# Attention: the row maxima of two heads in one pass, in pairs of PSUM banks

## The chip, the core and the metric

The kernel runs on one NeuronCore of a Trainium2 chip. The metric is the device time of one execution in microseconds (us); lower is better. Engines are named as the profile names them: PE is TensorE's matmul, PEld its weight load, DVE VectorE, ACT ScalarE, POOL GpSimd, SP SyncE.

## What is computed

Two layers of a diffusion trunk on 1024 latent tokens (`x`) and 256 context tokens (`ctx`), width 1024. Each layer has a mixer (attention with 8 query heads and 2 key/value heads of 64 channels beside a gated MLP, one output projection) and a SwiGLU FFN. Only the latents' attention and, in layer 0, the context's matter here:

```python
def latent_attention(q, k_all, v_all):        # k_all, v_all: 256 context + 1024 latent tokens
    ...
    def one_block(qblk):
        s = jnp.einsum("bkgqd,bksd->bkgqs", qblk, kt, preferred_element_type=jnp.float32) * scale
        p = jax.nn.softmax(s, axis=-1).astype(vt.dtype)
        return jnp.einsum("bkgqs,bksd->bkgqd", p, vt)
    ...
```

Context queries attend to the context's keys only. The last layer needs no context output.

## The kernel before, in words

Exactness comes from splitting each operand into a rounded part (hi, type fp32r) and the rest (lo): `rnd` (ACT, L118) rounds, `sub_lo` (DVE, L121) takes the rest. All matmuls go through `mm` (L112). SBUF and PSUM are handed out as slots by `Ring`; PSUM is eight slots of one bank each (`BK`), and a slot that is freed goes to the end of the queue. The instructions are written down in the order of the Python code; a list scheduler then sets the order on each engine by that order as priority and by what is ready. Nothing reorders them on the chip.

The attention of a layer works on 16 **units**: two groups of 512 queries by 8 heads. A unit has five **steps** of two key tiles of 128. A step (`step`, L830) makes the transposed logits of two key tiles, four matmuls of 512 columns into two banks: for each key tile Khi by the whole query (`st_k<-qT_p,kh_p` or `kc_p`), then Klo and a row of -1 by the rounded query and the row of maxima (`st_k<-q_p,kl_p`, 65 rows). So the maximum is subtracted inside the product. ACT takes the exponential of each bank by itself (L844, `pt_p<-st_k`), rounds both (`sp_b<-pt_p`, 1024 elements), DVE subtracts (`sp_b<-pt_p,sp_b`). The value products of a step (`values`, six matmuls of 512 columns, two of them 64 wide: `pv_k<-sp_b,vt_p 128*64`) are written two steps later (`run_values(2)`, L894).

The row maxima are made one unit ahead by the generator `prepare` (L698), which is advanced once per step. For a unit it makes the logits with the queries on the partitions: eight matmuls of 512 latent keys (`ml_k`, L718), each into a bank of its own and reduced by a DVE instruction of its own (L719), and four of 256 context keys (`mc_k`, L714), two to a bank with one reduction (L715). The stationary operand has 128 rows, Qhi over Qlo of one head, and the moving one is `[Khi; Khi]`. A last reduction (`m`, L725) joins the chunks, four transposes (`mt_k`, L730) bring the maxima into a row, and ACT rounds that row into the 65th row of `q2` (`q_p<-mt_k`, L731). The second product of the next unit's first step waits for this row. The first unit's `prepare` is advanced twice after each of the last three projections of the queries (L784 to L786) and drained before the first step (L888). In layer 0 a generator `side` runs the context's eight heads between the steps.

Of the kernel before, what the change touches and what calls it, by code (L numbers as in the profile page):

```python
# [10 lines left out]
F32 = mybir.dt.float32  # L11
# [6 lines left out]
P = 128  # L18
# [19 lines left out]
# columns of w_in in the order they are used: u, v (gMLP), k|v, q  # L38
# [3 lines left out]
class Ring:  # L42
    """Slots of one size in SBUF or PSUM, handed out first-freed first."""
# [12 lines left out]
    def part(self, n):  # L56
        """A ring of its own out of n free slots, until it's closed."""
        r = Ring(self.pool, 0, self.pfx, self.words)
        r.queue = [self.queue.pop(0) for _ in range(n)]
        r.up = self  # L60
        r.names = self.names
        return r

    def close(self):
        self.up.queue += self.queue
        self.queue = self.up.queue

# [10 lines left out]
class Share:  # L78
    """A view of a slot that several share; the last one to free it frees the slot."""
# [16 lines left out]
def trunk(ctx: ExitStack, tc, x, xctx, w_mod, b_mod, vecs, gqk, gsg, g_post, w_in, w_sT, w_out,  # L96
# [9 lines left out]
    BK = Ring(ps, 8, "k", 512)  # L106
# [16 lines left out]
    # ---- constants  # L123
# [10 lines left out]
    one_v = cst.tile([P, 2, 2], F32, name="one_v")     # a column of ones, as the first of two or as the second  # L134
# [7 lines left out]
    fm = cst.tile([P, 2, 2, 4, KT], F32, name="fm")   # [layer][x/ctx][a_mix, b_mix, a_ffn, b_ffn]  # L142
# [16 lines left out]
    # ---- modulation vectors  # L159
# [9 lines left out]
    def mods_first():  # L169
        """Shift and scale of the first norm, both streams at once: products, then columns."""  # L170
# [130 lines left out]
    def norm_early(xt):  # L301
        """Normed and transposed, before the modulation is known."""
# [53 lines left out]
    class Lag:  # L356
        """Work whose emission waits until n more pieces of work came behind it."""
# [13 lines left out]
    # ---- weights as a rounded part and the exact rest  # L371
# [21 lines left out]
    # ---- one layer  # L393
# [8 lines left out]
    class HT:  # L402
        """Normed activations, features on partitions, as stationary tiles: hi/lo [128, kt, 128] per token tile."""
# [6 lines left out]
        def next_l(self):  # L410
            """One more pair of tiles."""
# [49 lines left out]
    def gmlp_mix(l, vs, up, ws):  # L461
        """m = (W_s v + b_s) * u, in place of u."""
# [20 lines left out]
    def head_norm(src, nt, nh, tabA, tabB):  # L483
        """RMS norm over each head's 64 channels with gain and rotation folded into tabA/tabB; f32 result page."""
# [21 lines left out]
    def layer(l):  # L506
# [3 lines left out]
        # -- norms, gMLP  # L510
# [85 lines left out]
        for g, (kind, prs) in enumerate(groups):  # L596
            n = 2 * len(prs)
            vs[g] = [(PG.get([n, PC], F32R, "vh"), PG.get([n, PC], F32R, "vl")) for _ in range(2)]
            for k, pr in enumerate(prs):
# [37 lines left out]
        for kind, pr in [("c", 0)] + [("l", i) for i in range(4)]:  # L637
# [36 lines left out]
            v = PG.get([2, KVH, 3, HD], F32R, "vt")      # [Vhi | 1 | Vlo]  # L674
# [10 lines left out]
        # -- attention: units of (kind, group of query tiles, head)  # L685
# [12 lines left out]
        def prepare(u):  # L698
            """Row maxima of the logits, and [Qhi; max] as a moving operand; in steps."""
# [4 lines left out]
            mx = sm.tile([P, 4, 3], F32, name="mx", tag="mx")  # L704
# [809 lines left out]
```

## Time and profile before

| what | value |
| --- | --- |
| median of 3 runs | 2771.4 us (2771.33 to 2777.08) |
| the profiled execution | span 2767.1 us from its first to its last instruction; no time of its own is given |
| attention of layer 0, first to last value product | 303.7 to 556.7 us |
| attention of layer 1 | 1758.5 to 1989.8 us |
| busy share of the span, PE, DVE, ACT, POOL | 98%, 71%, 45%, 16% |

The profile gives times of one execution, in us from its first instruction. The median lies 4.3 us above the span: what lies outside the first and last instruction. A matmul's recorded duration runs from its start to the modelled end of its results, so it overlaps the next one; how fast matmuls follow each other is read from merged rows of several (the row's length less one duration, over the count less one). The same holds for ACT and DVE instructions, which overlap a little where they stand back to back.

### The profile page before, as it was taken

How to read it: one execution, taken by the hardware profiler on the slowest of the kernel's cores; microseconds unless marked ns; L12 is line 12 of the kernel's file. 1: busy time of each engine (PE TensorE's matmuls, PEld its weight loads, DVE VectorE, ACT ScalarE, POOL GpSimd, SP SyncE). 2: the span in 40 equal slices, each digit the busy share in tenths (PEclk: the TensorE clock that was granted, in tenths of full speed). 3: DMA queues.
4: the chain of work that ended last, by engine and by line, in shares of the span. 5: the costliest groups of instructions: out<-in, count | busy, mean ns of one | idle time of the engine just before them, and what ended most of it. 6: DMA issues, size and time to landing. Idle time of an engine off the chain costs nothing.

```text
span 2767.1 us, 36916 instructions
## 1 busy us (share of the span) xinstructions
PE 2719.3 (98%) x14257; PEld 2267.2 (82%) x14257; DVE 1970.5 (71%) x2806; ACT 1235.2 (45%) x2055; POOL 444.8 (16%) x463
## 2 busy tenths in 40 slices
PE   7999999999999999999999999999998999999998
PEld 4999777688888788888899999777787888888887
DVE  6775788857888897865688556888758666666544
ACT  5323788845333223411276323688744333335111
POOL 1112000003232332000010002000013232330003
PEclk9999999999999999999999999999999999999999
DMA  7330000233532434742376410001232212225223
GB/s 276 121 124 32 3 14 20 79 110 108 205 136 107 153 137 138 257 170 97 106 240 225 139 56 32 5 8 36 91 130 90 78 71 82 92 77 190 84 77 114
DMA packets 91614, 298.14 MB, mean 108 GB/s; under 512 B 20431, under 2 KB 21263, under 8 KB 86318
## 3 DMA queue, kind: packets, MB, share of 16 engines
q1 hardware_dynamic: 91438, 295.78, 30.5%
q8 instruction: 112, 1.84, 0.3%
q14 instruction: 64, 0.52, 0.1%
HBM read 249.96 MB, written 45.71 MB: 107 GB/s over the span
## 4 chain that ended last, share of the span: by engine, by line
PE 88%; ACT 4%; DMA 3%; DVE 3%; issue 1%; POOL 1%; SPq 0%; DVEq 0%; POOLq 0%; ACTq 0%
PE fi_k L112 34%; PE fo_k L112 19%; PE pz_k L112 6%; PE op_k L112 6%; PE pv_k L112 6%; PE st_k L112 4%; PE pq_k L112 4%; PE ml_k L112 2%; PE pkv_k L112 2%; ACT pt_p L115 1%; ACT sp_b L118 1%; PE mg_k L112 1%; PE hT_k L334 1%; PE m_k L112 1%; DMA wraw_p<-in_w_in_dram 1%
## 5 line engine op out<-in xcount | busy, mean ns | idle before, releaser
L112 PE MATMUL fi_k<-blk_p,fw_p 128*128 128x512 f32 x2640 | 608.0, 390 | 0.3 <-ACT blk_p L118 0.3
L112 PEld LDWEIGHTS fi_k<-blk_p,fw_p 128*128 128x128 f32 x2640 | 496.3, 188 | 104.7 <-issue 0.9
L112 PE MATMUL pv_k<-sp_b,vt_p 128*128 128x512 f32 (+2 forms) x1008 | 277.5, 394 | 5.0 <-DVE sp_b L121 4.0
L118 ACT ACTIVATE fw_p<-fir_b 128x512 fp32r<-128x512 f32 x200 | 126.1, 631 | 319.5 <-PE fi_k L112 304.1
L112 PE MATMUL fi_k<-blk_b,fw_p 128*128 128x512 f32 x1056 | 251.8, 395 | 0.4 <-DVE y_p L972 0.4
L286 POOL TENSOR_SCALAR rs<-ss 128x1 f32<-128x1 f32 x74 | 24.7, 333 | 1333.5 <-DVE ss L968 607.0
L112 PEld LDWEIGHTS fi_k<-blk_b,fw_p 128*128 128x128 f32 x1056 | 201.4, 191 | 42.9 <-DVE y_p L972 0.8
L121 DVE TENSOR_TENSOR sp_b<-pt_p,sp_b 128x1024 fp32r<-128x1024 f32 (+1 forms) x168 | 200.3, 1195 | 26.8 <-ACT sp_b L118 24.8
L112 PE MATMUL fo_k<-foh_p,foh_p 128*128 128x512 f32 x704 | 218.4, 390 | 0.0
L112 PE MATMUL fo_k<-fol_p,foh_p 128*128 128x512 f32 x704 | 218.0, 389 | 0.0
L112 PE MATMUL fo_k<-foh_p,fol_p 128*128 128x512 f32 x704 | 217.9, 389 | 0.0
L112 PEld LDWEIGHTS pv_k<-sp_b,vt_p 128*128 128x128 f32 (+1 forms) x1008 | 162.4, 170 | 62.9 <-DVE sp_b L121 11.4
L1246 DVE TENSOR_TENSOR acc_b<-fo_k,acc_b 128x512 f32<-128x512 f32 x176 | 113.1, 685 | 140.1 <-PE fo_k L112 140.1
L719 DVE TENSOR_REDUCE mx<-ml_k 128x1 f32<-128x512 f32 x256 | 168.1, 685 | 39.9 <-PE ml_k L112 39.2
L118 ACT ACTIVATE foh_p<-fo_b 128x1024 fp32r<-128x1024 f32 x88 | 90.6, 1058 | 227.4 <-PE fo_k L112 122.8
L112 PE MATMUL pz_k<-winh_p,hTl_b 128*128 128x256 f32 x1024 | 187.6, 285 | 0.2
L115 ACT ACTIVATE pt_p<-st_k 128x512 f32<-128x512 f32 (+1 forms) x336 | 180.6, 590 | 14.9 <-PE st_k L112 13.8
L121 DVE TENSOR_TENSOR fw_p<-fir_b,fw_p 128x512 fp32r<-128x512 f32 x200 | 176.7, 884 | 11.2 <-ACT fw_p L118 9.0
L234 DVE SCALAR_TENSOR_TENSOR macc_p<-wm_p,cT,macc_p 128x1024 f32<-128x1024 f32 x128 | 171.8, 1356 | 14.3 <-DMA wm_p<-in_w_mod_dram 11.8
L118 ACT ACTIVATE sp_b<-pt_p 128x1024 fp32r<-128x1024 f32 (+1 forms) x168 | 175.8, 1046 | 1.7
L112 PEld LDWEIGHTS pz_k<-winh_p,hTl_b 128*128 128x128 f32 x1024 | 161.0, 193 | 2.9 <-issue 0.9
L112 PEld LDWEIGHTS fo_k<-foh_p,foh_p 128*128 128x128 f32 x704 | 131.8, 188 | 28.7 <-DVE gp_p L247 0.9
(261 smaller groups left out, 5362.0 us busy)
## 6 DMA issues: line engine op xcount, KB each, us to landing
wm_p<-in_w_mod_dram SPq DMA_DIRECT2D x112, 512.0 KB
fir_b<-in_w_fi_dram SPq DMA_DIRECT2D x40, 1024.0 KB
fir_p<-in_w_fi_dram SPq DMA_DIRECT2D x52, 512.0 KB
hid<-hid_p SPq DMA_DIRECT2D x44, 512.0 KB
fo_b<-hid SPq DMA_DIRECT2D x44, 512.0 KB
fo_b<-in_w_fo_dram SPq DMA_DIRECT2D x44, 512.0 KB
wraw_p<-in_w_in_dram SPq DMA_DIRECT2D x28, 512.0 KB
for_p<-in_w_fo_dram SPq DMA_DIRECT2D x22, 512.0 KB
```

The lines of the kernel that those rows point to most:

```text
L112: nc.tensor.matmul(o, lhsT, rhs, start=start, stop=stop)
L115: A.activation(out=o, in_=i, func=f, **kw)
L118: A.activation(out=o, in_=i, func=AF.Copy)
L121: V.tensor_tensor(out=o, in0=i, in1=hi.bitcast(F32), op=ALU.subtract)
L234: V.scalar_tensor_tensor(out=accs[v].t, in0=w.t, scalar=cT[:, v, kt:kt + 1], in1=accs[v].t, op0=ALU.mult, op1=ALU.add)
L286: nc.gpsimd.tensor_scalar(out=y, in0=src, scalar1=float(eps), scalar2=1.0, op0=ALU.add, op1=ALU.mult)
L334: nc.tensor.transpose(bk.t[:, k, :], xs.t[:, (4 * q + k) * P:(4 * q + k + 1) * P], idn)
L719: V.tensor_reduce(out=mx[:, b, i:i + 1], in_=bk.t, axis=AX.X, op=ALU.max)
L1246: V.tensor_tensor(out=a, in0=bks[h].t, in1=a, op=ALU.add)
```

## The change

The line numbers of the changed kernel are those before plus 46 in the helpers, and a few more further down (`mm` is L158, `rnd` L164, `sub_lo` L167).

- PSUM becomes one tile of eight banks (`Banks`); `two` hands out an even bank and the next one as a pair. During the steps banks 6 and 7 are set apart for the value products (`PV`), so that three pairs are left for logits, maxima and transposes.
- The queries of the odd head of a pair are stored as lo over hi instead of hi over lo. `prepare` then works for two heads at once: head 0 on rows 0 to 63 of the array, head 1 on rows 64 to 127, Qhi by Khi alone, each into its own bank of a pair. One DVE instruction reduces both banks (1024 elements). The number of matmuls is the same.
- `prepare` is made once per pair of heads, for the pair that follows, with ten chunks and a last step; it is advanced once per step over the ten steps of two units. Eight transposes stand together, and one ACT instruction rounds the maxima of both heads (1024 elements of one partition); the copy of Qhi into `q2` is two ACT instructions instead of one.
- A step's logits lie in a pair of banks, and one ACT instruction takes the exponential of both.

```diff
-            if h % 2 == 0:
-                q2[kind, g, h // 2] = t = PG.get([2, nqb * P], F32R, "q2")
-                rnd(t.t[:HD], qp.t[:HD].bitcast(F32))
-            for n, (b, i) in enumerate(chunks):
+            q2[kind, g, h // 2] = t = PG.get([2, nqb * P], F32R, "q2")
+            for j in range(2):
+                rnd(t.t[:HD, j], qp.t[j * HD:(j + 1) * HD, j].bitcast(F32))
+            half = [slice(0, HD), slice(HD, P)]
+            for b, i in chunks:
                 if b == "c":
-                    bk = BK.get([2, CTX], F32, "mc")
+                    bk = BK.two([2, 2, CTX])
+                    for n in range(2):
+                        for j in range(2):
+                            mm(bk.t[:, j, n], qp.t[half[j], j, (2 * i + n) * P:(2 * i + n + 1) * P], kc.t[half[j], 0, kv, :], True, True)
+                    V.tensor_reduce(out=mx[:, :, 2 * i:2 * i + 2, 2], in_=bk.t, axis=AX.X, op=ALU.max)
+                else:
+                    bk = BK.two([2, 512])
                     for j in range(2):
-                        mm(bk.t[:, j], qp.t[:, h % 2, (2 * i + j) * P:(2 * i + j + 1) * P], kc.t[:, 0, kv, :], True, True)
-                    V.tensor_reduce(out=mx[:, 2 * i:2 * i + 2, 2], in_=bk.t, axis=AX.X, op=ALU.max)
-                else:
-                    bk = BK.get([512], F32, "ml")
-                    mm(bk.t, qp.t[:, h % 2, b * P:(b + 1) * P], kh[kv].t[:, i * 512:(i + 1) * 512], True, True)
-                    V.tensor_reduce(out=mx[:, b, i:i + 1], in_=bk.t, axis=AX.X, op=ALU.max)
+                        mm(bk.t[:, j], qp.t[half[j], j, b * P:(b + 1) * P], kh[kv].t[half[j], i * 512:(i + 1) * 512], True, True)
+                    V.tensor_reduce(out=mx[:, :, b, i], in_=bk.t, axis=AX.X, op=ALU.max)
                 bk.free()
-                if n % 2 == 1 and n < len(chunks) - 1:
-                    yield
+                yield
...
-                bks = [BK.get([nq], F32, "st") for _ in range(2)]
+                bk = BK.two([2, nq])
                 for k in range(2):
                     kt = 2 * k2 + k
-                    mm(bks[k].t, kslice(0, kv, kt), qa, True, False)
-                    mm(bks[k].t, kslice(1, kv, kt), qb, False, True)
-                    act(pt.t[:, k, :], bks[k].t, AF.Exp)
-                for bk in bks:
-                    bk.free()
+                    mm(bk.t[:, k], kslice(0, kv, kt), qa, True, False)
+                    mm(bk.t[:, k], kslice(1, kv, kt), qb, False, True)
+                act(pt.t, bk.t, AF.Exp)
+                bk.free()
...
+            PV = BK.part([6, 7])
             for n, u in enumerate(units):
-                pre = prepare(units[n + 1]) if n + 1 < len(units) else iter(())
+                if n % 2 == 0:
+                    pre = prepare(units[n + 2]) if n + 2 < len(units) else iter(())
```

Outside the attention and the end of the projection of the queries, the instructions of every engine stand in the same order as before. Two places inside show what moves.

DVE at the start of layer 1's attention, from the last norm of the queries (`qss`) to the first joined maximum (`m`). Before:

```order
L489 TENSOR_REDUCE qss<-sq_p_16426 128x8
L496 TENSOR_TENSOR qr_p_16433<-pq_k_16377,tab_p_15213 128x512
L498 TENSOR_TENSOR sq_p_16426<-pq_k_16377,tab_p_15213 128x8x32 x2
L715 TENSOR_REDUCE mx<-mc_k_16454 128x2
L500 TENSOR_TENSOR qr_p_16433<-qr_p_16433,sq_p_16426 128x512
L715 TENSOR_REDUCE mx<-mc_k_16458 128x2
L502 TENSOR_TENSOR qr_p_16433<-qr_p_16433,rs 128x512
L725 TENSOR_REDUCE m_16462<-mx 128x4
```

With the change, the same stretch (L769 reduces a pair of `ml` banks, L764 a pair of `mc` banks, L774 joins):

```order
L535 TENSOR_REDUCE qss<-sq_p_15202 128x8
L542 TENSOR_TENSOR qr_p_15209<-banks,tab_p_14039 128x512
L544 TENSOR_TENSOR sq_p_15202<-banks,tab_p_14039 128x8x32 x2
L769 TENSOR_REDUCE mx<-banks 128x2
L546 TENSOR_TENSOR qr_p_15209<-qr_p_15209,sq_p_15202 128x512
L769 TENSOR_REDUCE mx<-banks 128x2
L548 TENSOR_TENSOR qr_p_15209<-qr_p_15209,rs 128x512
L769 TENSOR_REDUCE mx<-banks 128x2
L167 TENSOR_TENSOR qst_p_15215<-qr_p_15209,qst_p_15215 128x4x128
L769 TENSOR_REDUCE mx<-banks 128x2
L764 TENSOR_REDUCE mx<-banks 128x2x2 x2
L774 TENSOR_REDUCE m_15272<-mx 128x8
```

Four reductions of `ml` pairs and one `sub_lo` come ahead of the joined maximum, and all six reductions take two banks.

PE at a border of two units of layer 1, around the transposes of the maxima (`idr,m`). Before (`st_k` are logits, `pv_k` values, `q_p` is `q2`):

```order
L112 MATMUL st_k_16780<-qT_p_16031,kh_p_15340 128x512
L730 MATMUL mt_k_16741<-idr,m_16739 1x128 x4
L112 MATMUL st_k_16781<-qT_p_16031,kh_p_15340 128x512
L112 MATMUL pv_k_16688<-sp_b_16728,vt_p_15785 128x512
L112 MATMUL pv_k_16688<-sp_b_16728,vt_p_15785 64x512
L112 MATMUL pv_k_16688<-sp_b_16728,vt_p_15785 128x512
L112 MATMUL st_k_16755<-q_p_16630,kc_p_15344 128x512
```

With the change, a border of two pairs of heads (`kc_p,qT_p` is the last quad of `mc`, `kh_p,qT_p` the next pair's first `ml`):

```order
L158 MATMUL banks<-kc_p_14168,qT_p_15142 128x256 x4
L158 MATMUL banks<-sp_b_15840,vt_p_14394 128x512
L158 MATMUL banks<-sp_b_15840,vt_p_14394 64x512
L158 MATMUL banks<-sp_b_15840,vt_p_14394 128x512 x2
L158 MATMUL banks<-sp_b_15840,vt_p_14394 64x512
L158 MATMUL banks<-sp_b_15840,vt_p_14394 128x512
L158 MATMUL banks<-qT_p_15142,kc_p_14168 128x512 x2
L780 MATMUL banks<-idr,m_15892 1x128 x8
L158 MATMUL banks<-kh_p_14164,qT_p_14976 128x512 x2
L158 MATMUL banks<-sp_b_15858,vt_p_14512 128x512
L158 MATMUL banks<-sp_b_15858,vt_p_14512 64x512
L158 MATMUL banks<-sp_b_15858,vt_p_14512 128x512
L158 MATMUL banks<-q_p_15700,kc_p_14168 128x512 x2
```

Eight transposes stand where four stood, one `ml` pair and three value products are left between them and the product that reads the row of maxima, and logits of the next step no longer stand among them.

## Rows read from the trace of the kernel before

**Rows 1.** The page: the span, and busy time of each engine.

```profile
span 2767.1 us, 36916 instructions
...
PE 2719.3 (98%) x14257; PEld 2267.2 (82%) x14257; DVE 1970.5 (71%) x2806; ACT 1235.2 (45%) x2055; POOL 444.8 (16%) x463
```

**Rows 2.** Busy time by stretch: attention of both layers, then their starts.

```profile
core 0: us, PE busy (x) PEld busy (x) DVE busy (x) ACT busy (x) POOL busy (x), PEclk, DMA share, GB/s
303.00:557.00 254.00, 248.33 (x1148) 180.29 (x1146) 212.24 (x295) 219.23 (x349) 0.00 (x0) 1.00 0.13 33
1758.00:1990.00 232.00, 230.04 (x1029) 166.30 (x1028) 197.31 (x266) 196.58 (x296) 0.00 (x0) 1.00 0.12 34
293.00:303.00 10.00, 8.28 (x30) 5.71 (x30) 7.05 (x14) 6.26 (x11) 1.84 (x2) 0.66 0.00 0
1745.00:1758.00 13.00, 11.99 (x46) 8.20 (x45) 9.48 (x17) 9.62 (x16) 1.83 (x2) 0.74 0.00 1
```

**Rows 3.** The tiles ml_k and mc_k: duration ns min/median/max, first and last start.

```profile
L112 PE MATMUL ml_k<-kh_p,qT_p x256: 387/396/755, 277.6 to 1967.3; 128*128 128x512 f32 x128
L112 PE MATMUL mc_k<-kc_p,qT_p x128: 274/282/366, 292.3 to 1969.6; 128*128 128x256 f32 x128
L112 PE MATMUL mc_k<-kc_p,qTc_p x16: 278/281/580, 296.0 to 375.8; 128*128 128x256 f32 x16
```

**Rows 4.** Timeline, steady steps of layer 1: start us, length us, instruction, [idle before].

```profile
1850.83 0.63 PE L112 MATMUL mc_k<-kc_p,qT_p 128*128 128x256 f32 x4
...
1852.76 1.07 ACT L118 ACTIVATE q_p<-qT_p 64x1024 fp32r<-64x1024 f32 x1
...
1853.71 1.06 ACT L118 ACTIVATE sp_b<-pt_p 128x1024 fp32r<-128x1024 f32 x1
...
1854.22 1.54 PE L112 MATMUL pv_k<-sp_b,vt_p 128*128 128x512 f32 x6
1854.69 0.68 DVE L719 TENSOR_REDUCE mx<-ml_k 128x1 f32<-128x512 f32 x1
1855.28 1.22 DVE L121 TENSOR_TENSOR sp_b<-pt_p,sp_b 128x1024 fp32r<-128x1024 f32 x1
...
1855.60 0.62 PE L112 MATMUL st_k<-qT_p,kh_p 128*128 128x512 f32 x2
```

**Rows 5.** Timeline, a border of two units in layer 1.

```profile
1838.02 2.39 DVE L121 TENSOR_TENSOR sp_b<-pt_p,sp_b 128x1024 fp32r<-128x1024 f32 x2
...
1840.40 1.28 DVE L719 TENSOR_REDUCE mx<-ml_k 128x1 f32<-128x512 f32 x2
...
1840.82 0.60 PE L730 MATMUL mt_k<-idr,m 128*1 128x128 f32 x4
...
1841.46 0.59 ACT L118 ACTIVATE q_p<-mt_k 1x512 fp32r<-1x512 f32 x1 [2.31 <-PE mt_k L730]
...
1842.19 0.64 PE L112 MATMUL st_k<-q_p,kc_p 65*128 65x512 f32 x2
...
1842.63 1.58 ACT L115 ACTIVATE pt_p<-st_k 128x512 f32<-128x512 f32 x3 [0.59 <-PE st_k L112]
```

**Rows 6.** Timeline, the start of layer 1's attention.

```profile
1743.76 0.28 PE L112 MATMUL pq_k<-winh_p,hTl_b 128*128 128x256 f32 x1
...
1743.88 0.79 PE L776 MATMUL qTp_k<-idr,qst_p 128*128 128x128 f32 x8
...
1744.71 0.69 DVE L489 TENSOR_REDUCE qss<-sq_p 128x8 f32<-128x512 f32 x1 [1.23 <-ACT sq_p L115]
...
1748.96 0.16 DVE L725 TENSOR_REDUCE m<-mx 128x4 f32<-128x12 f32 x1
...
1749.18 0.60 PE L730 MATMUL mt_k<-idr,m 128*1 128x128 f32 x4 [0.17 <-DVE m L725]
...
1750.45 0.80 PE L112 MATMUL st_k<-q_p,kc_p 65*128 65x512 f32 x1
```

**Rows 7.** Waits of PE in the steps, layer 1: us in total, times, longest.

```profile
PEld pv_k L112 <- DVE sp_b L121: 5.0, 12, 1.0
PEld st_k L112 <- ACT q_p L118: 3.1, 14, 0.4
```

**Rows 8.** The same waits in layer 0.

```profile
PEld pv_k L112 <- DVE sp_b L121: 6.5, 11, 1.9
PEld st_k L112 <- ACT q_p L118: 5.5, 18, 0.9
```

More of the change, by code (lines that the diff above doesn't have):

```diff
@@ L66, in close, with __init__, get, part @@
         self.queue = self.up.queue
+class Banks:
+    def __init__(self, pool, n):
+        self.t = pool.tile([P, n, 512], F32, name="banks")
+        self.queue = list(range(n))
+    def get(self, shape, dt=F32, name="t"):
+        return Bank(self, [self.queue.pop(0)], shape)
+    def part(self, at):
+        r = Banks.__new__(Banks)
+        r.t, r.up, r.queue = self.t, self, list(at)
+        self.queue = [i for i in self.queue if i not in at]
+        return r
+    def close(self):
+        self.up.queue += self.queue
+    def two(self, shape):
+        q = self.queue
+        i = min((i for i in q if i % 2 == 0 and i + 1 in q), key=lambda i: max(q.index(i), q.index(i + 1)))
+        q.remove(i)
+        q.remove(i + 1)
+        return Bank(self, [i, i + 1], shape)
+class Bank:
+    def __init__(self, banks, at, shape):
+        self.banks, self.at = banks, at
+        n = int(np.prod(shape)) // len(at)
+        t = banks.t[:, at[0], :n] if len(at) == 1 else banks.t[:, at[0]:at[0] + 2, :n]
+        if len(at) == 1 and len(shape) == 2:
+            t = t.rearrange("p (a b) -> p a b", b=shape[1])
+        if len(shape) == 3:
+            t = t.rearrange("p (a b c) -> p a b c", b=shape[1], c=shape[2]) if len(at) == 1 else t.rearrange(
+                "p a (b c) -> p a b c", c=shape[2])
+        self.t = t
+    def free(self):
+        self.banks.queue += self.at
+        self.t = None
 class Slot:
@@ L105, in trunk @@
     BG = Ring(sb, NBIG, "b", 4096)
-    BK = Ring(ps, 8, "k", 512)
+    BK = Banks(ps, 8)
     dma = nc.sync.dma_start
@@ L720, in prepare @@
                 bk.free()
-                if n % 2 == 1 and n < len(chunks) - 1:
-                    yield
+                yield
             if lat:
-                m4 = sm.tile([P, 4], F32, name="m4", tag="m4")
+                m4 = sm.tile([P, 2, 4], F32, name="m4", tag="m4", bufs=2)
                 V.tensor_reduce(out=m4, in_=mx, axis=AX.X, op=ALU.max)
             else:
-                m4 = mx[:, :, 2]
-            bk = BK.get([nqb, P], F32, "mt")
-            for b in range(nqb):
-                nc.tensor.transpose(bk.t[0:1, b, :], m4[:, b:b + 1], idn)
@@ L731, in prepare @@
-            rnd(q2[kind, g, h // 2].t[HD:HD + 1, h % 2, :], bk.t[0:1].rearrange("p a t -> p (a t)"))
+                m4 = mx[:, :, :, 2]
+            bk = BK.two([2, nqb, P])
+            for j in range(2):
+                for b in range(nqb):
+                    nc.tensor.transpose(bk.t[0:1, j, b, :], m4[:, j, b:b + 1], idn)
+            rnd(t.t[HD:HD + 1], bk.t[0:1].rearrange("p j a t -> p j (a t)"))
             bk.free()
@@ L757, in layer @@
                 rf = r.t.rearrange("p a h d -> p (a h) d")
-                rnd(st.t[:, :, 0:HD], rf)
-                sub_lo(st.t[:, :, HD:2 * HD], rf, st.t[:, :, 0:HD])
+                sv = st.t.rearrange("p (g h) (x d) -> p g (h x) d", h=2, x=2)
+                rg = rf.rearrange("p (g h) d -> p g h d", h=2)
+                rnd(sv[:, :, 0::3], rg)
+                sub_lo(sv[:, :, 1:3], rg, sv[:, :, 0::3])
                 r.free()
@@ L853, in values @@
                     if k2 == 0:
-                        pv[u] = BK.get([nq], F32, "pv")
+                        pv[u] = PV.get([nq], F32, "pv")
                     bk = pv[u]
@@ L872, in side @@
                     q = []
-                    drain(prepare(u))
+                    if h % 2 == 0:
+                        drain(prepare(u))
                     yield
@@ L895, in attention @@
                     next(more, None)
-                drain(pre)
+                if n % 2 == 1:
+                    drain(pre)
                 done(u)
@@ L900, in attention @@
             run_values(0)
+            PV.close()
             return outs
```

2 lines of the change are left out of this document (1 added, 1 removed).

## The prediction

> **What bounds the kernel now.** First the page: PE is busy 2719.3 of the span's 2767.1 us, DVE 71%, ACT 45% [rows 1]. That is the whole program, and the change touches its two attentions, so the next view is busy time by stretch [rows 2]. In layer 1's attention PE is busy 230.04 of 232 us, ACT 196.58 and DVE 197.31; in layer 0's 248.33, 219.23 and 212.24 of 254. The granted clock is 1.00 in both, the upper level (2.4 GHz). So PE bounds each stage, with two engines close behind at 85%: time saved on PE counts, but not without limit. The waits say where PE stood: for the rest of the probabilities (`sp_b`) 5.0 us in layer 1 and 6.5 in layer 0, for the row of maxima (`q_p`) 3.1 and 5.5 [rows 7, 8].
>
> Durations overlap, so costs are pitches from merged rows. Six value products take 1.54 us and one 0.39, so one follows another after (1.54 - 0.39) / 5 = 0.23 us; four `mc` take 0.63 and one 0.28: 0.12 us [rows 3, 4]. 512 columns at 2.4 GHz are 0.213 us; the other 0.017 I take as the change of weights.
>
> **Half the array.** The number of matmuls stays. 256 `ml` and 144 `mc`, of which 400 are listed [rows 3], now use 64 rows each, and by the order on PE 119 pairs of 512 columns and 67 of 256 stand with opposite halves next to each other; 24 stand alone. If the halves run side by side, the second of a pair costs only about 0.017: 119 x 0.213 + 67 x 0.103 = **-32.2 us**. If they don't, nothing is saved. No row of this trace shows two matmuls in different rows, so this is the largest unknown. What speaks for overlap is only that nothing in the operands forbids it: other rows, other banks. I take overlap.
>
> The Trainium skill ("TensorE: Matmul & The Clock Gate", Part 3) says that matmuls in different row groups run at once, 3.07 times faster for four of them; my estimate from that page is a tenth of a matmul for each further one, which would make the saving 31.2 us. No run here shows it yet.
>
> **DVE and ACT.** A reduction of 512 takes 0.60 us in a row of two (1.28 - 0.68) and a subtraction of 1024 1.17 (2.39 - 1.22) [rows 4, 5]; I take 1.17 for a reduction of two banks, between 1.13 and 1.20. So 256 x 0.60 become 128 x 1.17, 2% less. An exponential of 512 takes 0.53 in a row at most (1.58 / 3) [rows 5], a pass of 1024 elements 0.95 (1853.71 - 1852.76) [rows 4], so merging two gains ACT 0.1 us. Neither bounds: 0 us. The split copy of Qhi costs ACT a start more per head, hidden as long as ACT has its 15% free.
>
> **Start of each attention.** Here DVE decides. From the last norm of the queries to the joined maximum it works from 1744.71 to 1749.12 without a break [rows 6]. By the order it now has six reductions of two banks and one `sub_lo` there in place of two reductions: 6 x 1.17 + 0.60 - 2 x 0.60 = +6.4 us. Eight transposes for four: four take 0.60, so at most 0.60 more, taken 0.5; one rounding of 1024 for 512: 1.06 - 0.59 = +0.47 [rows 4, 5]. Against that eight transposes of queries that came after the first logits now lie in the gap: -0.8 [rows 6]. The `ml` and `mc` drawn into the gap are counted once, with the pairs. +6.6 per layer, **+13.2 us**. It can't be hidden behind other work: in the 13 us after the last projection PE has little to do even now and runs at a mean clock of 0.74 (0.66 in layer 0) [rows 2].
>
> **Borders.** Seven borders of head pairs per layer replace fifteen of heads. At one, the last `mc` quad is followed by a reduction (1.17), the join (0.16) and the transposes; ahead of that reduction on DVE may stand up to a whole subtraction (1.17). From the last matmul's start to the maxima that is 0.28 + 1.17 + 0.16 + 0.06 to 1.17 more, 1.67 to 2.84. The order gives PE six value products and two logits in that time: 0.12 + 8 x 0.23 = 1.96. PE waits 0 to 0.88. Then ACT rounds 1024 elements (1.06, behind up to 0.95 of another pass) while PE has only an `ml` pair and three value products (4 x 0.23 = 0.92): 0.2 to 1.15. The middle of both is 1.1 us, 14 times: +15.4. Gone are the waits of before for `q_p`, 3.1 + 5.5 x 14/18 = 7.4 (four of layer 0's 18 I count to the context, which stays) [rows 7, 8]. Net **+8.0 us**, bounds -4.6 and +21.
>
> **Pairs of banks.** One exponential waits for four products where each waited for two: 0.46 us later at most. The value products stand two steps later, which hides it but for the waits on `sp_b` that exist: 12 + 11 times [rows 7, 8], 23 x 0.46 = 10.6 as the upper bound, 0 as the lower. Layer 1's waits are short against the two steps' slack, so I take a quarter: **+2.5 us**.
>
> **Clock.** At the starts PE loses about (1 - 0.74) x 13 + (1 - 0.66) x 10 = 6.8 us to the lower level, 1.2 GHz [rows 2]. A longer gap can prolong that; bounds 0 and 6.8, taken **+2 us**, since the gaps grow by half and hold little PE work.
>
> Sum: -32.2 + 13.2 + 8.0 + 2.5 + 2 = -6.5 us on a span of 2767.1, so 2760.6. The median of the runs lies 4.3 us above that span: **2765 us**.
>
> **The rivals.**
>
> *Each switch drains the array* (slower). By the order the 400 half-row matmuls stand in 160 runs among full ones, 320 switches. Rows show that a change in columns costs nothing: two of the six value products at 0.23 are 64 wide [rows 4]. Of rows they show nothing: the 65-row logits follow each other in 0.64 - 0.39 = 0.25 [rows 5], but are still more than half. If the array must be empty before a switch, it costs up to 0.39 - 0.23 = 0.16 us, 51 us in all. It decides from 6.5 / 320 = 0.02 us on. At the middle, 0.08 a switch, a tenth of them in gaps: +23 - 6.5, 2788 us. For it: no row excludes it. Against it: nothing else in the trace that alternates shapes stalls. 0.20.
>
> The Trainium skill ("TensorEngine Tiling (Array Packing)", Key Properties) states that changing the tiling mode drains TensorE, which is this rival's rule; the 64-wide value products are such a change in columns, and the trace shows no drain at them, so that row speaks against the rule.
>
> *The halves don't overlap.* The saving is 0; start-ups and borders gain the matmuls moved into them (2 x 1.8 and 14 x 0.23), and neither clock nor exponentials cost anything, since PE stays further behind: 13.2 - 3.6 + 15.4 - 3.2 - 7.4 = +14.4, 2786 us. This is also the case in which the change does not do what it says. 0.13.
>
> *The new waits are hidden.* Borders at their lower bound (-4.6), pairs of banks and clock 0: -32.2 + 13.2 - 4.6 = -23.6, which would be 2748; with the two close engines in the way rather 2754. Against it: ACT has a pass of 1024 in its way at most times. 0.15.
>
> **How the numbers follow.** A difference under 0.2% (5.5 us) can't be told from none. The forecast has 0.52 and a range of its own, 2757 to 2772: the borders at 0.5 or 1.6 us, the clock at 0 or 6.8. Its middle lies at the edge of 0.2%, so about 0.29 of it is faster, 0.22 the same, the rest slower. With hidden waits (nearly all faster) and the two slow rivals, whose low ends reach down to no change (switches under 0.04 us; borders well covered): faster 0.43, same 0.30, slower 0.27. The range goes from 2752 to 2788, through most of the slow rivals; a full drain lies outside it.
>
> **What the new profile would show.** Right: the second of an `ml` pair starts within 0.03 us of the first, and a logits product after a pair not later than 0.25 after its last. PE's waits for `q_p` at borders about 0.6 us, and for `m` 0.4, 14 times; the first transpose of layer 1 some 12 us after the last `pq` instead of 5.4; ACT and DVE busier as a share, PE less. Wrong: pairs with 0.23 between starts (no overlap); 0.05 to 0.16 more ahead of or behind each half-row run (drain); waits on `sp_b` of more than 10 us per layer (the pairs of banks, or DVE, became the bound).

## The result and the profile after

The change made the kernel slower: 2799.1 us median (2797.6 to 2803.4) against 2772.8; the ratio is 1.0101, 95% interval 1.0086 to 1.0117. That lies outside the range, beyond the rival in which switches drain the array (2788 us). The profiled execution has a span of 2795.8 us, 28.7 more than before [rows 1]. Its time was 2797.6, 1.8 us above the span; the 4.3 us that the prediction put between span and median is more than lies outside the first and last instruction, so before's profiled run was probably some 2.5 us faster than its median.

The page of the changed kernel:

```profile
span 2795.8 us, 36626 instructions
...
PE 2737.9 (98%) x14257; PEld 2242.9 (80%) x14257; DVE 1958.9 (70%) x2626; ACT 1235.4 (44%) x1887; POOL 438.6 (16%) x463
```

PE is still the bound, with 18.6 us more busy time than before for the same number of matmuls. Where the 28.7 us came in is read from three marks in each layer: the last matmul of the query projections (`winh_p`), and the first and last value product (`sp_b,vt_p`). In the table, "start" is the time from the first of these marks to the second, "steps" from the second to the third, for the kernels that the text needs (before, the change, and the experiments that follow):

| us | before | change | e1 | e3 | e8 | e11 |
| --- | --- | --- | --- | --- | --- | --- |
| start, layer 0 | 12.15 | 25.51 | 23.94 | 27.01 | 22.60 | 14.32 |
| steps, layer 0 | 252.56 | 254.44 | 245.54 | 267.35 | 249.19 | 246.26 |
| start, layer 1 | 14.71 | 23.94 | 21.29 | 24.36 | 22.21 | 13.37 |
| steps, layer 1 | 230.98 | 236.04 | 224.77 | 253.67 | 229.90 | 224.76 |

The two starts take 22.6 us more, the steps 6.9; the rest of the program differs by 0.8 the other way. (Where layer 0's projections end varies by up to 4.4 us from before in these kernels, and the stretch between the layers by up to 5; these are not explained here. The profiled execution was the slowest of nine for e8, 3.5 us over its median, and the fastest of eight for e11, 3.7 us under it.)

A steady piece of layer 1 after the change, from the timeline:

```profile
1846.44 0.39 PE L158 MATMUL banks<-q_p,kl_p 65*128 65x512 f32 x1
1846.76 0.19 PEld L158 LDWEIGHTS banks<-kh_p,qT_p 64*128 64x128 f32 x2 [0.36 <-issue]
1846.76 0.51 PE L158 MATMUL banks<-kh_p,qT_p 64*128 64x512 f32 x2
...
1847.20 1.24 PEld L158 LDWEIGHTS banks<-sp_b,vt_p 128*128 128x128 f32 x6 [0.25 <-issue]
1847.20 1.67 PE L158 MATMUL banks<-sp_b,vt_p 128*128 128x512 f32 x6
```

Two matmuls of 64 rows take 0.51 us together, so they run side by side. But the first comes 0.32 after the product ahead of it, not 0.23; the value products come 0.44 after the pair, not 0.23; and six of them take 1.67, not 1.54 [rows 4]. The load of the first half-row matmul's weights (PEld) starts with the matmul, not one matmul ahead: 0.001 us before it, in the kernel of e1 below 0.229 us (medians of 88 places). PEld's waits in the steps of layer 1 and of layer 0, where "issue" means that nothing in the profile was waited for:

```profile
PEld banks L158 <- issue: 31.9, 106, 0.4
PEld banks L158 <- ACT sp_b L164: 4.2, 12, 0.6
PEld banks L158 <- DVE sp_b L167: 2.8, 3, 1.0
PEld banks L158 <- ACT q_p L164: 2.5, 8, 0.6
PEld banks L158 <- ACT pt_p L161: 2.1, 6, 0.5
...
PEld banks L158 <- issue: 28.9, 100, 0.4
PEld banks L158 <- ACT pt_p L161: 5.0, 11, 1.1
PEld banks L158 <- ACT sp_b L164: 4.1, 11, 0.4
PEld banks L158 <- ACT q_p L164: 2.5, 7, 0.7
```

Rows of the same view of the kernel before, layer 1:

```profile
PEld ml_k L112 <- ACT pt_p L115: 5.7, 22, 0.4
...
PEld pv_k L112 <- ACT pt_p L115: 2.0, 9, 0.3
PEld st_k L112 <- ACT pt_p L115: 2.0, 10, 0.2
...
PEld pv_k L112 <- ACT sp_b L118: 1.3, 3, 0.7
```

PE's wait for `sp_b` on DVE fell from 5.0 to 2.8 in layer 1, the wait for `q_p` from 3.1 to 2.5 in layer 1 and from 5.5 to 2.5 in layer 0 [rows 7, 8], those for `pt_p` in layer 1 from 9.7 to 2.1. The wait on data that rose most is that for `sp_b` on ACT, from 1.3 to 4.2 in layer 1. The data waits together fell; what is new in the steps is 206 times "issue".

The start of layer 1, timeline of the changed kernel:

```profile
1758.36 0.28 PE L158 MATMUL banks<-winh_p,hTl_b 128*128 128x256 f32 x1
...
1759.31 0.69 DVE L535 TENSOR_REDUCE qss<-sq_p 128x8 f32<-128x512 f32 x1 [0.45 <-ACT sq_p L161]
...
1768.84 2.36 DVE L764 TENSOR_REDUCE mx<-banks 128x4 f32<-128x1024 f32 x2 [1.25 <-PE banks L158]
...
1771.23 0.18 DVE L774 TENSOR_REDUCE m<-mx 128x8 f32<-128x24 f32 x1
...
1771.99 1.87 PE L780 MATMUL banks<-idr,m 128*1 128x128 f32 x8
...
1773.90 1.01 ACT L164 ACTIVATE q_p<-banks 1x1024 fp32r<-1x1024 f32 x1 [4.34 <-PE banks L780]
...
1774.96 1.22 PE L158 MATMUL banks<-q_p,kc_p 65*128 65x512 f32 x2 [0.38 <-ACT q_p L164]
...
1776.40 0.63 PE L158 MATMUL banks<-q_p,kl_p 65*128 65x512 f32 x1
...
1776.83 0.63 PE L158 MATMUL banks<-qT_p,kh_p 128*128 128x512 f32 x1
...
1782.30 1.05 PE L158 MATMUL banks<-sp_b,vt_p 128*128 128x512 f32 x2
```

The maxima are joined 13.0 us after the last projection instead of 5.4, and the first transpose comes at 13.6 [rows 6]. Busy time and granted clock by stretch (columns as in [rows 2]):

```profile
1758.00:1763.00 5.00, 3.57 (x30) 2.72 (x29) 4.38 (x8) 2.90 (x6) 1.83 (x2) 1.00 0.00 0
1763.00:1768.00 5.00, 2.35 (x15) 1.54 (x14) 4.59 (x5) 1.33 (x3) 0.00 (x0) 0.69 0.00 0
1768.00:1773.00 5.00, 4.12 (x12) 2.31 (x13) 2.53 (x3) 1.54 (x3) 0.00 (x0) 0.50 0.00 0
1773.00:1778.00 5.00, 4.62 (x13) 3.00 (x11) 1.23 (x1) 3.40 (x4) 0.00 (x0) 0.50 0.00 0
1778.00:1783.00 5.00, 4.03 (x11) 2.16 (x11) 2.57 (x3) 3.86 (x4) 0.00 (x0) 0.50 0.00 0
1783.00:1788.00 5.00, 5.00 (x17) 3.35 (x17) 3.79 (x4) 2.92 (x3) 0.00 (x0) 0.77 0.00 0
```

PE is busy 2.35 of 5 us while DVE works, then runs at 0.50, the lower level (1.2 GHz), until the first value products are through. There a logits product follows the one ahead of it after 0.43 us (1776.40 to 1776.83) instead of 0.23. By the trace's clock records the lower level lasted 20.4 us here and 23.9 in layer 0; before, 6.8 us in each.

### The profile page after: what moved, and what is told of

Its sections match the earlier page's. It is cut to its first block, busy times and chain, and to the rows that moved or that the text cites. A ratio compares the mean times of both kernels' runs of the same rounds, so it can differ in the third digit from the quotient of the medians.

```text
span 2795.8 us, 36626 instructions
## 1 busy us (share of the span) xinstructions
PE 2737.9 (98%) x14257; PEld 2242.9 (80%) x14257; DVE 1958.9 (70%) x2626; ACT 1235.4 (44%) x1887; POOL 438.6 (16%) x463
## 4 chain that ended last, share of the span: by engine, by line
PE 91%; DVE 3%; ACT 2%; DMA 2%; issue 1%; POOL 1%; SPq 0%; DVEq 0%; POOLq 0%; ACTq 0%
PE banks L158 89%; PE banks L380 1%; PE banks L780 1%; ACT pt_p L161 1%; DMA wraw_p<-in_w_in_dram 0%; ACT sp_b L164 0%; PE banks L829 0%; POOL rs L333 0%; DVE sp_b L167 0%; DVE mx L769 0%; DMA wor_p<-in_w_out_dram 0%; DMA wm_p<-in_w_mod_dram 0%; ACT ov_p L161 0%; DMA ov_p<-rd0l 0%; PE banks L709 0%
## 5 line engine op out<-in xcount | busy, mean ns | idle before, releaser
L158 PE MATMUL banks<-blk_p,fw_p 128*128 128x512 f32 x2640 | 608.4, 390 | 0.3 <-ACT blk_p L164 0.3
L158 PEld LDWEIGHTS banks<-blk_p,fw_p 128*128 128x128 f32 x2640 | 496.5, 188 | 105.0 <-ACT blk_p L164 0.9
L158 PE MATMUL banks<-winh_p,hTl_b 128*128 128x256 f32 x1792 | 332.8, 286 | 1.0 <-DVE hTl_b L167 0.5
L158 PEld LDWEIGHTS banks<-winh_p,hTl_b 128*128 128x128 f32 x1792 | 283.8, 193 | 5.0 <-issue 2.1
L158 PE MATMUL banks<-sp_b,vt_p 128*128 128x512 f32 (+2 forms) x1008 | 276.0, 404 | 2.4 <-DVE sp_b L167 1.8
L164 ACT ACTIVATE fw_p<-fir_b 128x512 fp32r<-128x512 f32 x200 | 126.0, 631 | 318.8 <-PE banks L158 303.5
L158 PE MATMUL banks<-winl_p,hTl_b 128*128 128x256 f32 x896 | 254.7, 284 | 0.0
L158 PE MATMUL banks<-blk_b,fw_p 128*128 128x512 f32 x1056 | 250.2, 393 | 2.7 <-DVE y_p L1029 2.7
L332 POOL TENSOR_SCALAR rs<-ss 128x1 f32<-128x1 f32 x74 | 21.3, 288 | 1368.3 <-DVE ss L1025 638.2
L158 PEld LDWEIGHTS banks<-blk_b,fw_p 128*128 128x128 f32 x1056 | 199.9, 190 | 44.9 <-DVE y_p L1029 3.1
L167 DVE TENSOR_TENSOR sp_b<-pt_p,sp_b 128x1024 fp32r<-128x1024 f32 (+1 forms) x168 | 198.7, 1195 | 48.7 <-ACT sp_b L164 48.3
L158 PEld LDWEIGHTS banks<-sp_b,vt_p 128*128 128x128 f32 (+1 forms) x1008 | 160.2, 171 | 81.5 <-issue 24.5
L158 PE MATMUL banks<-foh_p,foh_p 128*128 128x512 f32 x704 | 218.3, 390 | 0.0
L158 PE MATMUL banks<-fol_p,foh_p 128*128 128x512 f32 x704 | 217.9, 389 | 0.0
L158 PE MATMUL banks<-foh_p,fol_p 128*128 128x512 f32 x704 | 217.9, 389 | 0.0
L769 DVE TENSOR_REDUCE mx<-banks 128x2 f32<-128x1024 f32 x128 | 155.9, 1220 | 51.6 <-PE banks L158 36.8
L164 ACT ACTIVATE foh_p<-fo_b 128x1024 fp32r<-128x1024 f32 x88 | 90.7, 1060 | 227.3 <-PE banks L158 151.2
L167 DVE TENSOR_TENSOR fw_p<-fir_b,fw_p 128x512 fp32r<-128x512 f32 x200 | 176.6, 883 | 11.3 <-ACT fw_p L164 9.0
L164 ACT ACTIVATE sp_b<-pt_p 128x1024 fp32r<-128x1024 f32 (+1 forms) x168 | 172.4, 1039 | 3.6
```

The source lines that it names most:

```text
L158: nc.tensor.matmul(o, lhsT, rhs, start=start, stop=stop)
L164: A.activation(out=o, in_=i, func=AF.Copy)
L167: V.tensor_tensor(out=o, in0=i, in1=hi.bitcast(F32), op=ALU.subtract)
L332: nc.gpsimd.tensor_scalar(out=y, in0=src, scalar1=float(eps), scalar2=1.0, op0=ALU.add, op1=ALU.mult)
L769: V.tensor_reduce(out=mx[:, :, b, i], in_=bk.t, axis=AX.X, op=ALU.max)
```

## The experiments

Two theories stood against each other after the result. **S**: each passage between full-row and half-row use of the array costs PE time, more than the overlap returns; and the start of each attention is late. **B**: the later maxima at borders and the merged exponentials cost the time, and the halves are a gain.

**e1, full rows.** Two heads at once, pairs of banks and the order on PE stay; the array is used whole.

```diff
-            half = [slice(0, HD), slice(HD, P)]
+            half = [slice(0, P), slice(0, P)]
```

> The changed kernel, but each maxima matmul uses all 128 rows again (Qhi over Qlo, or Qlo over Qhi, by [Khi; Khi]); pairs of banks, paired reductions, merged exponentials, two heads at once and the order on PE stay. Theory S (each passage between full-row and half-row use of the array costs time, about 0.10 us in and 0.20 us out, and the overlap of the halves gives back 0.21 per pair): in the steps the trace of the changed kernel has 39.9 us at 139 runs' borders against 26.9 us of overlap, so 13 us go, and some 4 to 8 more at the two start-ups: 2778 to 2783 us. Rival B (the later maxima at borders and the merged exponentials cost the time, the halves are a gain): the overlap is lost, 2810 to 2826 us, or nothing changes, 2799.

Measured: 2773.9 us, ratio 1.0021 (1.0011 to 1.0031): as S has it, and below its range. B falls. In the profile the steps take 20.2 us less than with the change, the starts 4.2. A steady piece:

```profile
1829.80 0.40 PE L158 MATMUL banks<-q_p,kl_p 65*128 65x512 f32 x1
...
1830.03 0.63 PE L158 MATMUL banks<-kh_p,qT_p 128*128 128x512 f32 x2
...
1830.50 1.54 PE L158 MATMUL banks<-sp_b,vt_p 128*128 128x512 f32 x6
```

Theory S had counted 13 us in the steps, for the way into each run and out of it; it had no term for the matmul behind each run (the table of e3).

**e2, half rows in the kernel before.** One edit to before's `ml` and `mc` (the line for `ml` is shown, that for `mc` is narrowed alike); it leaves Qlo by Khi out of the maxima.

```diff
-                    mm(bk.t, qp.t[:, h % 2, b * P:(b + 1) * P], kh[kv].t[:, i * 512:(i + 1) * 512], True, True)
+                    mm(bk.t, qp.t[:HD, h % 2, b * P:(b + 1) * P], kh[kv].t[:HD, i * 512:(i + 1) * 512], True, True)
```

> The kernel before with one edit: its maxima matmuls use rows 0 to 63 alone (Qhi by Khi), so the product Qlo by Khi is left out of the maxima. Nothing can overlap, and nothing else changes; by the order on PE the 400 half-row matmuls stand in 199 runs. Theory S: 199 x 0.29 to 0.40 us = 58 to 80 us, less what falls into waits: 2820 to 2850 us. Rival B: a matmul of 512 columns takes as long on 64 rows as on 128, 2773 us.

Measured: 2836.1 us, ratio 1.0249 (1.0234 to 1.0265). S, and the cleanest sign of it: the kernel before, with half the rows in 400 of its 14,257 matmuls and nothing else changed, takes 67 us more. Its timeline:

```profile
1850.99 0.61 PE L112 MATMUL st_k<-qT_p,kc_p 128*128 128x512 f32 x2
...
1851.54 0.73 PE L112 MATMUL ml_k<-kh_p,qT_p 64*128 64x512 f32 x2
...
1852.19 1.65 PE L112 MATMUL pv_k<-sp_b,vt_p 128*128 128x512 f32 x6
```

**e3, both heads on the same half.** The order on PE and the 160 runs of half-row matmuls stay; nothing can overlap.

```diff
-            half = [slice(0, HD), slice(HD, P)]
+            half = [slice(0, HD), slice(0, HD)]
```

(with Qhi over Qlo for odd heads too)

> The changed kernel with both heads of a pair on rows 0 to 63 (Qhi over Qlo for odd heads too), in the same order on PE, with the same 160 runs of half-row matmuls: the switches stay, the overlap goes. Theory S: 119 pairs of 512 columns and 67 of 256 no longer run side by side, 119 x 0.21 + 67 x 0.10 = +32 us, 2831 us, more if the second weight load of a pair isn't hidden (0.10 each, up to 2850). Rival C (PE isn't what the pairs wait for, their overlap is worth nothing in the steps): 2799 to 2805 us.

Measured: 2830.7 us, ratio 1.0230 (1.0215 to 1.0245). S: the steps take 30.5 us more than with the change, so the overlap is real and PE does wait for these matmuls. A pair there takes 0.73 us:

```profile
1862.43 0.40 PE L158 MATMUL banks<-q_p,kl_p 65*128 65x512 f32 x1
...
1862.76 0.73 PE L158 MATMUL banks<-kh_p,qT_p 64*128 64x512 f32 x2
```

e1, the change and e3 have the same pieces: a full matmul of 512 columns, a pair of `ml`, two full ones. From the single records of the trace, which the timeline merges, medians of the distances between starts in ns (over 88 such places in each of these three kernels):

```
                          into 1st half   to 2nd   to full   to next full   sum
e1, 128 rows                   233          237       233        230         933
the change, two halves         330            3       429        336        1098
e3, one half twice             331          338       324        332        1325
```

So a run with one pair costs 0.39 us without overlap (1.325 - 0.933), and overlap returns 0.227: +0.165 net. A run of four `mc`, two pairs of 256 columns, costs 1.331 - 0.949 = 0.38 and gets back 0.23 in the same way. With 103 and 33 such runs in the order on PE: 103 x 0.165 + 33 x 0.153 = 22 us, against 24.4 between e1 and the change in the starts and steps of the table. The other 24 of the 160 runs are not in this sum; 13 of them are a single half-row matmul, which in e2 costs 0.38 to 0.39 us too, with nothing back.

**e4, the first pair earlier.** Four chunks instead of two after each of the last three projections.

```diff
-                    for _ in range(2):
+                    for _ in range(4):
                         next(first, None)
```

> The changed kernel with the first pair's maxima advanced four chunks after each of the last three projections instead of two, so that all ten chunks and the transposes are written down before the last projections end. Theory S with its second part (the late first maxima cost 13.0 us in layer 0 and 8.9 us in layer 1, since six chunks were advanced where ten are needed): the time from the last projection to the first value product returns to 12 to 15 us, 2777 to 2783 us. Rival D (DVE has no room during the projections, whose norms are then late, or the wait moves into the steps): 2793 to 2799 us.

Measured: 2792.5 us, ratio 1.0088 (1.0073 to 1.0103), which overlaps the change's own interval. That is rival D: the starts took 18.7 us less by the trace, but the layer's last projection came later, by 8.3 and 4.6 us. DVE has 4.1 us of norms per projection and now four reductions of 1.13; PE runs dry and then works at the lower clock:

```profile
1735.00:1741.00 6.00, 6.00 (x55) 6.00 (x54) 3.56 (x8) 2.21 (x4) 1.84 (x2) 1.00 0.01 3
1741.00:1747.00 6.00, 4.86 (x33) 3.67 (x32) 4.33 (x8) 2.70 (x5) 1.83 (x2) 0.97 0.00 0
1747.00:1753.00 6.00, 6.00 (x41) 6.00 (x40) 4.58 (x5) 0.63 (x1) 0.00 (x0) 0.75 0.00 0
```

**e5, full rows, the first pair spread wider.** Three chunks after each of the four projections of the latents' second half of heads.

```diff
-                if q == 1 and kind == "l" and pr >= 1:
-                    for _ in range(2):
+                if q == 1 and kind == "l":
+                    for _ in range(3):
```

> The changed kernel with the maxima on all 128 rows (as in the first experiment) and the first pair's maxima spread over four projections of the queries, three chunks after each, instead of two chunks after each of three. Theory S: without switches what is left over the kernel before is the start of each attention, 23.9 and 21.3 us from the last projection to the first value product against 12.2 and 14.7; that returns to 13 to 15 each, and the projections, with 4.1 us of norms and 3.4 of reductions on DVE in their 7.3 us, lose 0 to 4: a ratio to the kernel before of 0.995 to 0.998, 2757 to 2765 us where before takes 2770, faster than both kernels. Rival D (as the third part of the last call showed: what the start gains, the projections lose on DVE): 1.000 to 1.002, 2769 to 2775.

Measured: 2767.6 us, ratio 0.9989 (0.9978 to 1.0000). Between the two forecasts, and its interval reaches the kernel before's time. By the trace layer 1's start fell from 21.3 to 13.4 us, with steps as in e1; layer 0's fell to 11.1, and its steps rose from 245.5 to 254.9.

**e6, runs twice as long.** Half rows as in the change; two chunks after every second step.

```diff
-                    next(pre, None)
+                    if (5 * (n % 2) + k2) % 2 == 0:
+                        for _ in range(2):
+                            next(pre, None)
```

> The changed kernel with the maxima advanced two chunks after every second step instead of one after each: by the order on PE the 400 half-row matmuls stand in 117 runs instead of 160. Theory S: 43 runs less at 0.29 to 0.40 us, -12 to -17 us: a ratio to before of 1.004 to 1.006 instead of 1.010, 2781 to 2787 us where before takes 2770. Rival E (with three pairs of banks, of which the maxima then hold two, logits wait for reductions): 1.010 or more, 2798 us or more.

Measured: 2786.6 us, ratio 1.0058 (1.0043 to 1.0073): S. Fewer passages with the same half-row matmuls cost less. In its 35 runs of two `ml` pairs between full matmuls of 512 columns the medians of the distances are 321, 3, 331, 4, 323 and 334 ns, 1.316 us for what takes six times 0.233, 1.40, on full rows: with two pairs a run gains 0.08 us, with one it loses 0.165. Its 12 runs of eight `mc` gain 0.10.

**e7, both.** e6 with the first pair spread as in e5.

> Both: half rows in runs of two chunks, and the first pair spread over four projections. Theory S: 119 runs, so the same 12 to 17 us, and 10 to 18 at the starts: a ratio to before of 0.997 to 1.002, 2762 to 2776 us where before takes 2770; the half-row form is then at best even with the kernel before. Rivals D and E: 1.006 or more.

Measured: 2781.0 us, ratio 1.0033 (1.0017 to 1.0048): slower than S said. The starts fell to 11.2 and 14.5 us, but layer 1's steps rose from 227.9 to 231.3 and layer 0's from 253.3 to 255.1, and the projections came later. The half-row form did not reach the kernel before.

**e8, the exponentials apart.** e1 with one exponential per bank.

```diff
-                act(pt.t, bk.t, AF.Exp)
+                    act(pt.t[:, k], bk.t[:, k], AF.Exp)
```

> The first experiment's kernel (maxima on all 128 rows) with one exponential per bank again, as in the kernel before; banks are still taken in pairs. What the merged exponential does by itself. The prediction charged it 2.5 us (0 to 10.6) for waiting for four products: then undoing it gives 2771 us (2763 to 2774) against 2774 of the first experiment. Theory A (it is a gain: ACT is 85% busy, two of 512 take 0.1 us longer than one of 1024, and PE's waits in the steps are 7.6 us shorter in the first experiment than in before): 2777 to 2784.

Measured: 2780.2 us, ratio 1.0032 (1.0022 to 1.0042). Its steps take 8.8 us more than e1's by the trace, as theory A had it; the ratios of the whole differ by 0.0011 (3 us), within their intervals, and the profiled execution was e8's slowest. So within this form the merged exponential is a gain in the profiled steps, and that it costs 2.5 us finds no support; how much it is worth stays open.

**e9, the merged exponential alone**, in the kernel before: one head at a time, four banks for logits, two for maxima, two for values.

```diff
+            PV = BK.part([6, 7])
+            mb[0] = BK.part([4, 5])
...
-                bks = [BK.get([nq], F32, "st") for _ in range(2)]
+                bk = BK.two([2, nq])
```

> The kernel before with one part of the change: a step's logits lie in a pair of banks and one exponential takes both. The maxima are made as before (128 rows, one head at a time, single banks, the first head's started as before); four banks are set apart for logits, two for maxima and two for values. Theory A (the merged exponential is the gain within the change: undoing it in the full-row kernel cost 8.8 us in the steps of the trace, 3.7 in layer 0 and 5.1 in layer 1, and the starts are untouched): a ratio to before of 0.996 to 0.998, 2759 to 2765 us where before takes 2770, faster than before and than the change. Rival F (the gain needs three pairs for the logits; with two, a step's logits wait for the exponential of the step two before): 1.000 or more. The prediction's term (+2.5 us) would give 1.001.

Measured: 2786.9 us, ratio 1.0062 (1.0048 to 1.0076). Theory A's forecast missed, but the run doesn't decide about the merged exponential, since it also leaves the maxima only two banks. In layer 1 the weight loads waited for these:

```profile
PEld banks L158 <- DVE mx L766: 9.8, 19, 1.3
PEld banks L158 <- DVE sp_b L167: 8.3, 16, 1.0
```

Rival F's number came, not its mechanism: PEld's waits for an exponential (`pt_p`) are 1.8 us in that layer.

**e10, three pairs, one head at a time.** To give the maxima more room: chunks of two banks of one head, five per unit.

```diff
...
+            for b in (range(nqb) if lat else []):
+                bk = BK.two([2, 512])
+                for i in range(2):
+                    mm(bk.t[:, i], qp.t[:, h % 2, b * P:(b + 1) * P], kh[kv].t[:, i * 512:(i + 1) * 512], True, True)
+                V.tensor_reduce(out=mx[:, b, 0:2], in_=bk.t, axis=AX.X, op=ALU.max)
...
```

> What the runs so far would keep of the change: pairs of banks and merged exponentials with three pairs for logits, maxima and transposes, as in the change, but the maxima of one head at a time on all 128 rows, five chunks of two banks with one reduction each, started as in the kernel before. No switches, no overlap, and as much DVE work ahead of the first maxima as before (5 x 1.17 against 10 x 0.60). Theory A: the steps keep what the full-row kernel gained by the merged exponentials (8.8 us in its steps) and the starts stay at 12 to 15 us: a ratio to before of 0.996 to 0.998, 2759 to 2765 us where before takes 2770. Rival F (as in the last run, where two banks alone for the maxima cost 19 us of PE's waits for their reductions: pairs held by maxima and transposes of a head at a time come back too late): 1.001 or more.

Measured: 2788.1 us, ratio 1.0050 (1.0036 to 1.0064): rival F. Its starts are as short as before (11.1 and 12.4 us), but its steps take 260.0 and 243.3. In layer 1:

```profile
PEld banks L158 <- ACT pt_p L161: 12.7, 41, 0.7
PEld banks L158 <- ACT sp_b L164: 7.8, 14, 0.6
PEld banks L158 <- DVE sp_b L167: 5.8, 17, 1.0
PEld banks L158 <- ACT q_p L164: 4.8, 15, 0.4
```

The 41 waits on `pt_p` are for banks whose exponential is late. With two heads at once (e1) there are 4; but the kernel before has 41 as well, of 9.7 us, and the wait that rose most beside it is that for `sp_b` on ACT, from 1.3 to 7.8. The rows of e1:

```profile
PEld banks L158 <- ACT q_p L164: 3.0, 7, 0.6
PEld banks L158 <- DVE sp_b L167: 2.9, 4, 1.0
PEld banks L158 <- ACT pt_p L161: 1.5, 4, 0.5
```

Which difference does it, fifteen borders for seven or transposes that hold a pair for one head each, was not separated.

**e11, the best of these.** e5, with layer 0's first maxima two chunks after each of five projections.

```diff
-                if q == 1 and kind == "l":
-                    for _ in range(3):
+                if q == 1:
+                    for _ in range(3 if last else 2):
```

> The fifth experiment's kernel (two heads at once on 128 rows, merged exponentials, first maxima spread over the projections), with layer 0's first maxima advanced two chunks after each of five projections (the context's too) instead of three after each of four; layer 1 stays at three after each of four. Theory S: in the fifth experiment layer 1 got back the 7 to 8 us that its start had lost, while layer 0 got back 12.9 at the start and lost most of it in the projections ahead (DVE) and in its first units; with two reductions of two banks per projection (2.3 us beside 4.1 of norms in 7.3) the projections lose nothing: 3 to 5 us less than the fifth, a ratio to before of 0.997 to 0.9985. Rival G (the first units of layer 0 are slow because the clock is at its lower level after the start, whatever the projections do): 0.9985 to 1.0.

Measured: 2764.7 us, ratio 0.9976 (0.9966 to 0.9987), as S has it: faster than the kernel before by a little, and than the change by 1.2%. The starts are 14.3 and 13.4 us, the steps 246.3 and 224.8, and the granted clock is 1.00 in both starts (e1: 0.72 and 0.76). Its interval overlaps e5's, so that e11 beats e5 isn't shown.

## Why the prediction was wrong

**Half the array: the overlap was right, the price of getting there was left out.** The forecast took -32.2 us for the pairs and nothing for the switches. The overlap is there: the second of a pair starts 3 ns after the first, and it returns 0.227 us per run of one `ml` pair or four `mc`; 136 such runs make 31 us. The step that failed is that a half-row run costs nothing besides: it costs 0.39 us, three times about 0.10 us in e3 and e2 (into the run, out of it, and at the next full matmul) and once more between two matmuls of the same half. 136 runs make 53 us. With 31 back, the term is +22 (e1: +24.4) where -32.2 stood. (By the trace 119 pairs of 512 columns and 64 of 256 start together and 34 matmuls stand alone; the prediction's own counts, 119 and 67 pairs, leave 28 alone, not 24. That changes its term by 0.3 us.)

The rival had the place of the cost and its count, and the signs set for it came: 0.32 for 0.23 ahead of a run, 0.44 for 0.23 behind. It took up to 0.16 us a switch, with the middle, 0.08, for its time; measured are 0.39 us for the two switches of a run, 0.195 each, above its upper end. Its argument against, that 64-wide value products cost nothing, speaks of columns: rows behave otherwise. The Trainium skill's rule ("TensorEngine Tiling (Array Packing)", Key Properties: changing the mode drains the engine) agrees with the trace for rows in that a switch costs time, 0.10 us into a run and 0.20 out of a pair; the 64-column products at 0.23 us [rows 4] show none of it. That the cost is a drain is not shown, since half of it falls one matmul behind the switch (last section). I let a row on columns speak for rows.

**Starts: right place, too small.** +13.2 us were forecast, and 2 for the clock; without switches e1 has 18.4 (23.94 + 21.29 less 12.15 and 14.71), with them 22.6. DVE's own work was sized right. From the norm to the joined maximum it took 12.1 us in both layers, instead of 4.4 in layer 1 and 3.2 in layer 0 (where before joined its first maxima ahead of the last two passes of the norm); without DVE's waits for `mc`, 1.25 and 2.39, that is +6.4 and +6.5 against +6.4.

Two parts were missed. One is these waits, 3.6 us, for which the prediction had no term. The other is what follows the join: the first value product came 10.9 us after the joined maximum, before 9.3 in layer 1; in layer 0 11.5 instead of 7.1. That is +6.0, where the prediction had 0.2 per layer and 2 for the clock. The lower level lasted 44 us in and just behind the two starts instead of 14, and products of 512 columns follow each other at 0.43 us in it. The prediction said that PE has little to do there; the rows that it names have PE busy 11.99 of 13 us, at a mean clock of 0.74 [rows 2].

Only six of ten chunks are advanced before the last projection ends, so four are left and stand in line behind the last norms. e5 and e11 undo it and bring the starts back to 11 to 14 us.

**Borders and pairs of banks: wrong sign.** +8.0 and +2.5 us were forecast. e8, with paired banks and one exponential per bank, has steps of 479.1 us in both layers against 483.5 before; 3.9 of the 4.4 are matmuls that now stand ahead of the steps (their columns, at 0.23 us per 512). So the borders with eight transposes, together with what else e8 keeps (reductions of two banks, banks in pairs), cost nothing net. The waits agree. In e1, with full rows, PEld waits 3.0 us for `q_p` in layer 1 (row above), and in layer 0:

```profile
PEld banks L158 <- ACT q_p L164: 4.6, 9, 1.3
...
PEld banks L780 <- DVE m L774: 0.8, 1, 0.8
```

That is 7.6 us for `q_p` against 8.6 before [rows 7, 8], and of the 14 waits of 0.4 us for `m` that were forecast two came, 1.0 us together. The merged exponential then took 8.8 off in the profile. The prediction charged each border the middle of its bounds; the net lay at 0, between that and the lower end (-4.6).

Sum of the measured parts in the profile: +24.4 (halves, e1 to the change) + 18.4 (starts without them) - 13.2 (steps of e1 against before) = 29.6, less 0.8 elsewhere: 28.8, against 28.7 in the spans. The sum goes from before to e1 and from e1 to the change, so it must close; it divides the loss and proves nothing by itself. What the parts mean rests on e2, e3 and e6 for the halves, and on e5 and e11 for the starts.

## What to carry to other kernels

Half-row matmuls side by side pay only in long runs, because the price is by the run: here a run pays some 0.39 us, one pair of 512 columns gets 0.23 back, and a run came out ahead only with two such pairs (by 0.08) or four of 256 columns (by 0.10), with four banks to hold it. When work is batched (two heads instead of one), count how much of the first batch must now be done before anything can start, and advance it earlier by as much; then check that the engine that does it (here DVE) has that room. When a row of the trace is held against a rule, make sure that it is about the same thing.

## What was not expected of the hardware

Two matmuls of 512 columns and 64 rows in the same half follow each other after 0.338 us, with 128 rows after 0.237. So half the rows made the second matmul later, not earlier, when nothing ran beside it. The load of its weights started 0.107 us after the matmul ahead had started, with 128 rows 0.002 us after (medians of 88 places in e3 and e1). In the waits this shows as 114 of PEld put down to "issue" in the steps of layer 1 of e3, where e1 has none:

```profile
PEld banks L158 <- issue: 41.0, 114, 0.7
```

It is not every half-row matmul that pays. Medians of the distances between starts, in ns, as in the table of e3:

```
                                     into   inside run    to full   to next full
e2, one matmul (37 places)            327   -               428         337
e2, two in the same half (83)         327   337             323         337
e3, four of 256 columns, one half     330   223 118 117     206         337
e6, two pairs, two halves each        321   3 331 4         323         334
```

Count two halves side by side as one place in the row. Then in all these kernels the first and the second place after a switch come about 0.10 us late, into half rows as well as out of them, and the third doesn't. A run with one place, be it one matmul or one pair, passes its second delay on to the full matmul behind it, which then comes after 0.43 instead of 0.32. So the price is 0.38 to 0.39 us per run, however much the run holds. Why a switch delays two places is not shown.
